# Forms of x at even multiples of 64 bytes with rows 34 to 54 units apart, weights at odd ones; a product of the linear branch's second half moved forward

## The chip, the cores and the metric

The kernel runs on one core of one Trainium2 chip. The metric is the device time of one execution in microseconds (us); runs of one kernel are summarised by their median. TensorE (PE, with its weight loads shown as PEld), VectorE (DVE), ScalarE (ACT) and GpSimd (POOL) work side by side. SyncE (SP) and POOL issue the transfers (DMA) from memory (HBM) into the on-chip buffer. A matmul has two operands there: the stationary one, which is loaded ahead of it, and the moving one, which streams past; its result goes to accumulators that ACT and DVE evacuate.

## The reference

One layer of a decoder: 512 rows of 1,024 numbers with 16 meta rows ahead of them, a retention branch of 4 heads and a gated linear branch (GLA) of 4 heads, merged by sigmoid gates and projected back.

```python
u = rms_norm(h, norm_gain)
proj = u @ w_in
(rq, rk, rv, rg, gq, gk, gv, gg, glr, m_ret, m_gla) = jnp.split(proj, points, axis=-1)
rq = rope(rq, pos); rk = rope(rk, pos) * RET_QK_DIM ** -0.5
o_ret = head_group_norm(retention_chunked(rq, rk, rv), ret_norm_gain) * jax.nn.silu(rg)
log_a = jax.nn.log_sigmoid(glr @ w_gate_up + b_gate) / GLA_GATE_TAU
o_gla = head_rms_norm(gla_chunked(gq * GLA_K_DIM ** -0.5, gk, gv, log_a), gla_norm_gain) * jax.nn.silu(gg)
merged = jax.nn.sigmoid(m_ret) * (o_ret @ w_branch_ret) + jax.nn.sigmoid(m_gla) * (o_gla @ w_branch_gla)
out = rms_norm(h + merged @ w_out, final_norm_gain)[:, N_META:]
```

## The kernel before

**Products in two parts.** Every number of an operand is held as a high part (fp32r) and a low part, the rest. ACT makes the high part by a cast and DVE the low part by a subtraction (`split`, L154), and each product is three matmuls: high by high, high by low, low by high. A matmul multiplies 128 by 128 by 256 (or 264 with 8 meta rows); a few are 512 wide.

**Quads.** `quad` (L257 and following) multiplies x, cut into four blocks of 264 or 256 rows by 512 columns (A11, A12, A21, A22), by a block of weights of 1,024 rows by 512 columns, with 7 products instead of 8 (Strassen's scheme in Winograd's form). Its operands on x's side are seven *forms*: A11, A12, A22 and the sums S1, S2, S3, S4. A product has 24 matmuls (two column tiles by four slices of 128 by three), all of L318, so a quad has 168. Its weights arrive in pieces named w11, w21, x3, x1, w22; some are added up by DVE (L359, L369, L372, L379) or by a transfer that accumulates, issued on POOL (L282). Products are taken in the order A11, A12, S2, S3, S1, A22, S4, and, where `early` is set (the linear branch's projection bg only), A11, S3, S2, A12, S1, A22, S4. Results stand in three accumulators a, b, c: ACT copies one (`copy`, L334), and the caller's `evac` adds.

Two kinds of quad matter. In quads *with rows* (gg0, gg1, gv1; rg0 to rg3 and rv0 to rv3 of the four retention heads; wo1 of the last projection) the form is the stationary operand and the weights move. In the others (gqk1, mr0, mr1, mg0, mg1, rqk0 to rqk3, bg0, bg1) the form moves and the weights are stationary. gq0, gk0, gv0 (L643) at the start and wo0 and wo2 at the end multiply without the scheme; gv0 and wo0 and wo2 have the form stationary too. In the profile xh, xl are the tiles with A11, A12, A22 (and A21) of x, high and low; fh, fl those with the sums; `NAME_h`, `NAME_l` the two parts of a piece of weights; `NAME_a`, `_b`, `_c` the accumulators.

**Where the forms lie.** The pool `cp` gives its tiles out in the order of the code, so that sizes fix addresses. Counted in units of 64 bytes from the start of a partition's row, as worked out from these sizes, before:

| Operand | Start (high part) | From one slice of 128 to the next |
|---|---|---|
| A11, A21, A12, A22 of x | 75, 92, 211, 228 | 34 |
| S1, S2, S3, S4 of x | 619, 687, 755, 823 | 17 |
| the three weight slots, high; low | 1607, 1671, 1735; 1799, 1863, 1927 | 16 |
| forms of bg: A11; A12, S1, S2, S4 | 2081; 2338, 2598, 2730, 2858 | 16 |
| forms of bg in two pieces: S3, A22 | even | 16 |
| forms of wo1 (high parts): A11, A12, A22; S1, S2, S3, S4 | 211, 2293, 2309; 619, 687, 755, 823 | 32; 16 |

The low parts of x's forms lie 272 units further for A and S alike. So A11 and A12 are odd in all slices, A22 and A21 even in all, and the four sums alternate; weights are odd, and so are the high parts of wo1's forms.

**The linear branch's second half.** `gla_branch` runs bg0 and then bg1 over the output of the linear attention. That output arrives in pieces: `gla_sums` forms bg's seven operands (names ga11, ga12, ga22h/l, gs1, gs2, gs3h/l, gs4) step by step while the quads run, with S4's last, after an accumulating transfer into og (L1118, POOL), by a scaled copy on ACT (L1128) and a subtraction on DVE (L1129). `after` fixes the order of two instructions on an engine without a wait. Each engine runs its own list in order; `weave` and the generators' `yield` set how two strands are mixed.

Of the kernel before, what the change touches and what calls it, by code (L numbers as in the profile page):

```python
# [21 lines left out]
F32 = mybir.dt.float32  # L22
# [6 lines left out]
P = 128  # L29
# [18 lines left out]
E_U, E_D, E_A, E_B, E_END, E_ND = range(6)  # L48
A11, A12, A22, S1, S2, S3, S4 = range(7)


# [57 lines left out]
def hybrid_kernel(ctx: ExitStack, tc: tile.TileContext, I, out: bass.AP):  # L109
# [18 lines left out]

    xh = [cp.tile([P, 4, 2, HW], F32R, tag=f"xh{i}", name=f"xh{i}") for i in range(2)]
    xl = [cp.tile([P, 4, 2, HW], F32R, tag=f"xl{i}", name=f"xl{i}") for i in range(2)]  # L130
    ah = {(th, kh): xh[kh][:, :, th] for th in range(2) for kh in range(2)}
    al = {(th, kh): xl[kh][:, :, th] for th in range(2) for kh in range(2)}
    fh = [ah[0, 0], ah[0, 1], ah[1, 1]]
    fl = [al[0, 0], al[0, 1], al[1, 1]]
    fh += [cp.tile([P, 4, HW], F32R, tag=f"fh{i}", name=f"fh{i}") for i in range(3, 7)]
    fl += [cp.tile([P, 4, HW], F32R, tag=f"fl{i}", name=f"fl{i}") for i in range(3, 7)]

# [30 lines left out]
    def vec(ins):  # L168
        return queue("vec", ins)
# [87 lines left out]
    def quad(cols, rows, name, evac, meta=None, adds=True, ahead=False, behind=None, src=None,  # L257
             forms=None, wide=False, sooner=False, early=False):

# [65 lines left out]
        def copy(x, n):  # L325

            y = xc.tile([P, 2, HT], F32, tag="xc", name=f"{name}_x{n}")
            if wide:
                w = HT if n < 3 else 256
                for t in range(2):  # L330
                    nc.scalar.copy(y[:, t, :w], x[t][:, :w])
                return y
            y = y.rearrange("p t c -> p (t c)")[:, :512].rearrange("p (t c) -> p t c", t=2)
            nc.scalar.copy(y, x[2])  # L334
            return y
# [327 lines left out]
    for n in range(NTB):  # L663
        act(nc.scalar.activation(xr[n], xr[n], AF.Square, accum_out=ss[:, n:n + 1]))
        if n == 2:
            for s in range(2):
# [14 lines left out]
                             rt.unsqueeze(2).to_broadcast([P, NTB + 1, P])))  # L681
    vec(nc.vector.scalar_tensor_tensor(u01, u00, -1.0, u01, op0=ALU.mult, op1=ALU.subtract))

    def form(i, x):
        act(nc.scalar.copy(fh[i][:, :, :HT], x))

        def rest():
            vec(nc.vector.tensor_sub(fl[i][:, :, :HT], x, fh[i][:, :, :HT].bitcast(F32)))

        return rest  # L690
# [40 lines left out]
    def forget_gates():  # L731
# [114 lines left out]
    def gla_g(p):  # L846
        sg = g1.tile([P, NTB, 512], F32, tag="gsg", name=f"gsg{p}")
        G["sg", p] = sg

        def evac(n, th, x, y):  # L850
            total(sg[:, 2 * th:2 * th + 2, n * 256:(n + 1) * 256], x, y)

        yield from quad((C_GG + p * 512, C_GG + p * 512 + 256), True, f"gg{p}", evac,
                        sooner=p == 0)

# [244 lines left out]
    def gla_sums():  # L1100
# [24 lines left out]
        gform(A22, a11, list(low))  # L1125
        yield
        hi, lo = gforms[S4]
        after(nc.scalar.mul(hi, a00, -1.0), low[0])  # L1128
# [25 lines left out]
    def gla_branch():  # L1154

        cnt = [0]

        def evac(n, th, p, q):
            pool, tag = ((g1, "gvm"), (g1, "gsum"), (gp, "gk"))[cnt[0] % 3]
            t = pool.tile([P, 2, 256], F32, tag=tag, name=f"gb{cnt[0]}")  # L1160
# [9 lines left out]

        for j in range(2):
            yield from quad((j * 512, j * 512 + 256), False, f"bg{j}", evac, src=I["w_branch_gla"],
                            forms=[[gforms[i][x] for i in range(7)] for x in range(2)], early=True)

# [89 lines left out]
    def ret_g(h):  # L1264
        sg = rp.tile([P, NTB, 512], F32, tag="sg", name=f"sg{h}")
        R["sg", h] = sg
# [3 lines left out]
    def ret_v(h):  # L1270
        vh = rp.tile([P, NTB, 512], F32R, tag="vh", name=f"vh{h}")
        vl = rp.tile([P, NTB, 512], F32R, tag="vl", name=f"vl{h}")
        R["v", h] = vh, vl
# [23 lines left out]
    def ret_scores(h):  # L1297
        qh, ql, kh, kl = R["qk", h]
        dec = rp.tile([P, 2, T], F32, tag="dec", name=f"dec{h}")
        nc.sync.dma_start(dec, I["decay"][h])  # L1300
        sh = rp.tile([P, 1280], F32R, tag="sh", name=f"sh{h}")
        sl = rp.tile([P, 1280], F32R, tag="sl", name=f"sl{h}")
# [26 lines left out]
    def ret_attention(h):  # L1329
# [4 lines left out]
        if h == 0:  # L1334
            nc.gpsimd.memset(rp.tile([P, 16], F32, name="gap"), 0.0)
        oh, ol = [(rp if h < 3 else cp).tile([P, 4, T], F32R, tag=f"o{n}" if h < 3 else f"x{n}0", name=f"o{n}{h}")
                  for n in "hl"]
        R["o", h] = oh, ol
# [109 lines left out]
    for h in range(4):  # L1448
# [14 lines left out]
    mh, ml = [[cp.tile([P, 4, T], F32R, tag=f"x{n}1", name=f"m{n}0"),  # L1463
               rp.tile([P, 4, T], F32R, tag=("sg", "vl")[n == "l"], name=f"m{n}1")] for n in "hl"]
    sums = [[cp.tile([P, 4, 256], F32R, tag=f"f{n}{i}", name=f"ms{n}{i}") for i in range(3, 7)] for n in "hl"]
    mforms = [[m[0][:, :, :256], m[1][:, :, :256], m[1][:, :, 256:], *x] for m, x in zip((mh, ml), sums)]

# [37 lines left out]

    weave(ret_branches(), residual(), skip=14)


# [105 lines left out]
```

## Time and profile before

| | |
|---|---|
| Median of 3 runs | 757.08 us (756.8 to 758.7) |
| The profiled execution's own time | 759.11 us |
| Its span, from the first to the last instruction | 757.3 us |
| TensorE's granted clock, mean | 0.998 |
| HBM over the span | 153 GB/s |

The page gives for each engine its busy time, its share of the span and its count of instructions, and the chain of work that ended last. A row of the timeline is a start, a duration, the engine, the line, the operation and its operands, with the idle time before it and what ended that in brackets. Durations of PE's matmuls overlap, since one is still draining while the next streams; how fast they follow one another is read from their starts. A row of the groups gives a count, the busy time and the mean of one. A row of the windows gives for a stretch each engine's busy time and count.

### The profile page before, as it was taken

The page shows a single profiled execution, that of the slowest core. Times are in us where ns is not written, and L with a number is a line of the kernel's source. Part 1 is how long each engine was busy: PE and PEld are TensorE (multiplying, and loading weights), DVE is VectorE, ACT ScalarE, POOL GpSimd, SP SyncE. Part 2 cuts the span into 40 slices and gives each one's busy share as a digit, 9 for nine tenths or more (in the row PEclk, how much of TensorE's full clock was granted, in tenths as well). Part 3 has the DMA queues.
Part 4 walks back from the last instruction along what each step waited for, and adds up shares of the span by engine and source line. Part 5 has one row for each costly group of instructions (what it writes and reads, how often), then busy time and mean ns, then how long its engine had stood idle before and what let it go on. Part 6 is the DMA issues. An engine that isn't in the chain of part 4 may idle for free.

```text
span 757.3 us, 14065 instructions
## 1 busy us (share of the span) xinstructions
PE 748.2 (99%) x5595; PEld 701.3 (93%) x5595; DVE 609.2 (80%) x873; ACT 450.4 (59%) x764; POOL 138.8 (18%) x173
## 2 busy tenths in 40 slices
PE   9999999999999999999999999999999999999996
PEld 6799899999999999999989999989999999988996
DVE  6699877679897789789957688966787989775994
ACT  7897584666974466556546555646464756532562
POOL 2211110101221122110530100440011210111142
PEclk9999999999999999999999999999999999999999
DMA  9863421821589972733783562795476356687503
GB/s 301 286 141 78 118 63 50 195 85 57 130 182 272 305 165 88 168 112 133 199 249 117 120 159 86 204 223 136 130 166 145 107 144 189 227 194 210 128 29 112
DMA packets 100138, 117.42 MB, mean 155 GB/s; under 512 B 5732, under 2 KB 90852, under 8 KB 99816
## 3 DMA queue, kind: packets, MB, share of 16 engines
q1 hardware_dynamic: 79896, 88.19, 36.7%
q0 software_dynamic: 19888, 27.79, 20.3%
q8 instruction: 44, 0.72, 0.4%
q10 hardware_dynamic: 288, 0.53, 0.2%
q14 instruction: 22, 0.18, 0.1%
HBM read 104.44 MB, written 11.53 MB: 153 GB/s over the span
## 4 chain that ended last, share of the span: by engine, by line
PE 86%; DVE 6%; ACT 2%; DMA 2%; issue 2%; POOL 1%; POOLq 0%; DVEq 0%; ACTq 0%
PE rqk_b L318 6%; PE rv_b L318 6%; PE rg_b L318 6%; PE rqk_c L318 5%; PE br_p L193 3%; PE br_p L189 3%; PE br_p L192 3%; PE gg_b L318 3%; PE gv_p L643 3%; PE mg_b L318 3%; PE rv_c L318 3%; PE rg_c L318 3%; PE mr_b L318 2%; PE bg_b L318 2%; PE gg_c L318 2%
## 5 line engine op out<-in xcount | busy, mean ns | idle before, releaser
L189 PE MATMUL br_p<-oh,br_h 128*128 128x512 f32 x128 | 50.0, 390 | 0.0
L193 PE MATMUL br_p<-oh,br_l 128*128 128x512 f32 x128 | 50.0, 390 | 0.0
L192 PE MATMUL br_p<-ol,br_h 128*128 128x512 f32 x128 | 49.8, 389 | 0.0
L154 ACT CAST rv_h<-rv_w 128x1024 fp32r<-128x1024 f32 x24 | 25.3, 1052 | 27.2 <-DVE rv_w L372 9.6
L154 DVE TENSOR_TENSOR rv_l<-rv_w,rv_h 128x1024 fp32r<-128x1024 f32 x24 | 29.3, 1221 | 9.2 <-ACT rv_h L154 9.2
L154 DVE TENSOR_TENSOR rg_l<-rg_w,rg_h 128x1024 fp32r<-128x1024 f32 x20 | 24.4, 1220 | 8.3 <-ACT rg_h L154 8.3
L154 ACT CAST rg_h<-rg_w 128x1024 fp32r<-128x1024 f32 x20 | 21.0, 1052 | 15.6 <-PE br_p L192 6.0
L282 POOL DMA_DIRECT2D rqk_x<-in_w_in_dram x8 | 10.4, 1302 | 105.4 <-DVE rv_l L154 80.6
L193 PEld LDWEIGHTS br_p<-oh,br_l 128*128 128x128 f32 x128 | 24.0, 188 | 5.2
L192 PEld LDWEIGHTS br_p<-ol,br_h 128*128 128x128 f32 x128 | 24.0, 188 | 4.7
L189 PEld LDWEIGHTS br_p<-oh,br_h 128*128 128x128 f32 x128 | 24.1, 188 | 4.5
L154 ACT CAST rqk_h<-rqk_w 128x1024 fp32r<-128x1024 f32 x20 | 21.1, 1053 | 11.5 <-PE rqk_c L318 2.9
L154 ACT CAST br_h<-br_w 128x1024 fp32r<-128x1024 f32 x16 | 16.8, 1050 | 18.7 <-PE br_p L192 9.5
L154 DVE TENSOR_TENSOR rqk_l<-rqk_w,rqk_h 128x1024 fp32r<-128x1024 f32 x20 | 24.4, 1221 | 3.9 <-ACT rqk_h L154 3.8
L1354 ACT ACTIVATE on<-av,nm,g_r 128x512 f32<-128x512 f32 x16 | 12.5, 779 | 25.3 <-DVE nm L1352 25.3
L318 PE MATMUL rv_b<-rv_l,fh 128*128 128x256 f32 x96 | 27.1, 282 | 0.2 <-DVE rv_l L154 0.2
L318 PE MATMUL rqk_b<-fh,rqk_h 128*128 128x256 f32 (+1 forms) x96 | 27.2, 283 | 0.0
L318 PE MATMUL rqk_b<-fh,rqk_l 128*128 128x256 f32 (+1 forms) x96 | 27.1, 282 | 0.0
L318 PE MATMUL rqk_b<-fl,rqk_h 128*128 128x256 f32 (+1 forms) x96 | 27.1, 282 | 0.0
L318 PE MATMUL rg_b<-rg_h,fl 128*128 128x256 f32 x96 | 27.0, 281 | 0.0
L318 PE MATMUL rv_b<-rv_h,fl 128*128 128x256 f32 x96 | 27.0, 281 | 0.0
L318 PE MATMUL rg_b<-rg_l,fh 128*128 128x256 f32 x96 | 26.9, 280 | 0.0
(721 smaller groups left out, 3260.8 us busy)
## 6 DMA issues: line engine op xcount, KB each, us to landing
rv_w<-in_w_in_dram SPq DMA_DIRECT2D x16, 512.0 KB, 4.2
br_w<-in_w_branch_ret_dram SPq DMA_DIRECT2D x16, 512.0 KB, 3.4
rqk_w<-in_w_in_dram SPq DMA_DIRECT2D x12, 512.0 KB, 4.8
rg_w<-in_w_in_dram SPq DMA_DIRECT2D x12, 512.0 KB, 4.5
rqk_x<-in_w_in_dram SPq DMA_DIRECT2D x8, 512.0 KB, 4.0
rqk_x<-in_w_in_dram POOLq DMA_DIRECT2D x8, 512.0 KB, 8.0
rg_x<-in_w_in_dram SPq DMA_DIRECT2D x8, 512.0 KB, 3.7
rg_x<-in_w_in_dram POOLq DMA_DIRECT2D x8, 512.0 KB, 7.8
```

The source lines that it names most:

```text
L154: return nc.scalar.copy(hi, src), nc.vector.tensor_sub(lo, src, hi.bitcast(F32))
L189: m = nc.tensor.matmul(o, lh, rh, start=first, stop=False)
L192: nc.tensor.matmul(o, lh, rl, start=False, stop=False)
L193: m = nc.tensor.matmul(o, ll, rh, start=False, stop=last)
L282: x = nc.gpsimd.dma_start(t, block(0, 1), accum_op=ALU.add)
L318: m = nc.tensor.matmul(ps[t][:, :n] if wide else ps[t], l, r, start=first and j == 0, stop=kk == 3 and j == 2, skip_group_check=not fresh ...
L643: m = nc.tensor.matmul(pss[t], (al if j == 1 else ah)[t // 2, kh][:, k, c], (lo if j == 2 else hi)[:, kk, :], start=q == kk == j == 0, sto ...
L1354: nc.scalar.activation(on, ps, AF.Identity, scale=r, bias=nm)
```

## The change

Two things change.

First, places. The tiles of x are laid out anew as x0, x1, x2 (high and low of each): x0 holds A11 and A21 (S4 later lies in A21's place), x1 A12, A22 and S1, x2 S2 and S3. Two unused gaps (16 and 112 numbers) shift what follows. Every form starts at an even multiple of 64 bytes, and its slices lie 34 units apart in x0 (A11 at 76, S4 at 94), 54 in x1 (348, 366, 384) and 38 in x2 (780, 798). The weight slots move to 1535, 1599, 1663 and 1727, 1791, 1855, 16 apart, odd as before. bg's forms move by 72 units, so A11's is odd and the others even as before. The merged rows and their sums before the last projection (`mforms`) lie at 348, 2222, 2238, 76, 140, 484 and 780, even too. S1 and S4 of x now hold 256 rows, without the meta rows that they never needed. Since S4 lies in A21's place, it can be made only when gk0 no longer needs A21: its sum (L682 before) goes to another place, and its two parts are made after gg0's fifth product.

Second, the order in bg. bg1's first product (A11) comes ahead of bg0's S2. Its accumulator's copy goes to a tile of its own (`home`), and the evacuated results alternate between two tiles. `gla_sums` yields once more before S4.

The core of the diff:

```diff
+    gap(cp, 16, "gap0")
+    x0, x1, x2 = [[cp.tile([P, 4, w], F32R, tag=f"x{n}{i}", name=f"x{n}{i}") for n in "hl"]
+                  for i, w in enumerate((544, 864, 608))]
+    gap(cp, 112, "gap1")
...
+    fh, fl = [[a[0, 0], a[0, 1], a[1, 1], b[:, :, 576:832], c[:, :, :288], c[:, :, 288:576], z[:, :, 288:]]
+              for a, z, b, c in zip((ah, al), x0, x1, x2)]
...
+            if home and n == 1:
+                y = home()
+                nc.scalar.copy(y, x[2])
+                return y
...
             product(7, S3, x3, c, True)
-            nc.vector.tensor_add(w11, w11, x3)
+            w = nc.vector.tensor_add(w11, w11, x3)
+            if home:
+                after(w, low[1])
...
-    vec(nc.vector.scalar_tensor_tensor(u01, u00, -1.0, u01, op0=ALU.mult, op1=ALU.subtract))
-
-    def form(i, x):
-        act(nc.scalar.copy(fh[i][:, :, :HT], x))
+
+    def form(i, x, prev=None):
+        w = 256 if i in (S1, S4) else HT
+        h, l, x = fh[i][:, :, :w], fl[i][:, :, :w], x[:, :, :w]
+        y = nc.scalar.copy(h, x)
+        if prev:
+            after(y, prev[0])
+        else:
+            act(y)
...
-        forms.append(form(S4, u01))
-        for i in (2, 0, 1, 3):
+        for i in (2, 0, 1):
             forms[i]()
+        vec(nc.vector.scalar_tensor_tensor(u10, u00, -1.0, u01, op0=ALU.mult, op1=ALU.subtract))
...
+        if p == 0:
+            yield from islice(products, 4)
+            next(products)
+            form(S4, u10, low)()
+            yield
...
-            pool, tag = ((g1, "gvm"), (g1, "gsum"), (gp, "gk"))[cnt[0] % 3]
+            pool, tag = (g1, "gvm") if cnt[0] == 5 else ((g1, "gsum"), (gp, "gk"))[cnt[0] % 2]
...
+        def home():
+            return g1.tile([P, 2, 256], F32, tag="gvm", name="bg1_x1")
+
+        def half(j):
+            return quad((j * 512, j * 512 + 256), False, f"bg{j}", partial(evac, j), src=I["w_branch_gla"],
+                        forms=[[gforms[i][x] for i in range(7)] for x in range(2)], early=True,
+                        home=home if j else None)
+
+        a, b = half(0), half(1)
+        yield from run(islice(a, 2), islice(b, 1), a, b)
...
+    def rows4(t, o, w, c):
+        return t[:, o:o + 4 * w].rearrange("p (k c) -> p k c", k=4)[:, :, :c]
+
+    m0 = [cp.tile([P, 3456], F32R, tag=f"x{n}1", name=f"m{n}0") for n in "hl"]
+    mh, ml = [[rows4(t, 0, 544, T), rows4(rp.tile([P, w], F32R, tag=g, name=f"m{n}1"), o, 544, T)]
+              for n, t, g, w, o in zip("hl", m0, ("sg", "vl"), (2304, 2176), (16, 0))]
...
+    for n, m, t in zip("hl", (mh, ml), m0):
+        s23 = cp.tile([P, 2176], F32R, tag=f"x{n}0", name=f"ms{n}0")
+        s4 = cp.tile([P, 2432], F32R, tag=f"x{n}2", name=f"ms{n}2")
+        mforms.append([m[0][:, :, :256], m[1][:, :, :256], m[1][:, :, 256:], rows4(t, 2176, 288, 256),
+                       rows4(s23, 0, 256, 256), rows4(s23, 1024, 256, 256), rows4(s4, 0, 288, 256)])
```

On PE the change of order is one product that moves. Before, where S3 of bg0 ends (gs3h1, gs3l1 by the weights' piece 7), S2 of bg0 follows (gs2 by piece 6):

```order
L318 MATMUL bg0_c_2667<-gs3h1_2507,bg0_7_h_2701 128x256
L318 MATMUL bg0_c_2667<-gs3l1_2509,bg0_7_h_2701 128x256
L318 MATMUL bg0_c_2667<-gs3h1_2507,bg0_7_l_2702 128x256
L318 MATMUL bg0_b_2665<-gs2_2505,bg0_6_h_2730 128x256 x2
L318 MATMUL bg0_b_2665<-gs2_2505,bg0_6_l_2731 128x256
```

After the change, at the same place:

```order
L328 MATMUL bg0_c_2663<-gs3h1_2503,bg0_7_h_2697 128x256
L328 MATMUL bg0_c_2663<-gs3l1_2505,bg0_7_h_2697 128x256
L328 MATMUL bg0_c_2663<-gs3h1_2503,bg0_7_l_2698 128x256
L328 MATMUL bg1_b_2738<-ga11_2497,bg1_1_h_2741 128x256 x2
L328 MATMUL bg1_b_2738<-ga11_2497,bg1_1_l_2742 128x256
```

bg1's A11 (ga11 by bg1's piece 1) stands there now, 24 matmuls of it, and bg0's S2 follows it.

On DVE, in the middle of bg0, before. L369 adds up weights, L154 makes low parts (of ga22, of the weights' pieces 4, 3 and 1), L1167 and L1165 are evacuations, L1129 is S4's form:

```order
L369 TENSOR_TENSOR bg0_w21_2654<-bg0_w21_2654,bg0_w11_2653 128x1024
L154 TENSOR_TENSOR ga22l0_2512<-og1gk_2521,ga22h0_2510 128x512
L154 TENSOR_TENSOR ga22l1_2513<-og1gk_2521,ga22h1_2511 128x512
L1167 TENSOR_TENSOR gb0_2792<-bg0_a_2666,bg0_x1_2696 128x512
L154 TENSOR_TENSOR bg0_4_l_2832<-bg0_w21_2654,bg0_4_h_2831 128x1024
L154 TENSOR_TENSOR bg0_3_l_2860<-bg0_w22_2657,bg0_3_h_2859 128x1024
L1165 SCALAR_TENSOR_TENSOR gb1_2824<-bg0_b_2665,bg0_x3_2795 128x512
L1129 SCALAR_TENSOR_TENSOR gs4_2503<-og0_1331,gs4_2503 128x1024
L154 TENSOR_TENSOR bg1_1_l_2911<-bg1_w11_2895,bg1_1_h_2910 128x1024
```

After the change:

```order
L385 TENSOR_TENSOR bg0_w21_2650<-bg0_w21_2650,bg0_w11_2649 128x1024
L164 TENSOR_TENSOR bg0_5_l_2832<-bg0_x1_2652,bg0_5_h_2831 128x1024
L164 TENSOR_TENSOR ga22l0_2508<-og1gk_2517,ga22h0_2506 128x512
L164 TENSOR_TENSOR bg0_4_l_2873<-bg0_w21_2650,bg0_4_h_2872 128x1024
L164 TENSOR_TENSOR ga22l1_2509<-og1gk_2517,ga22h1_2507 128x512
L1198 TENSOR_TENSOR gb0_2835<-bg0_a_2662,bg0_x1_2692 128x512
L164 TENSOR_TENSOR bg0_3_l_2901<-bg0_w22_2653,bg0_3_h_2900 128x1024
L1160 SCALAR_TENSOR_TENSOR gs4_2499<-og0_1327,gs4_2499 128x1024
L1196 SCALAR_TENSOR_TENSOR gb1_2869<-bg0_b_2661,bg0_x3_2838 128x512
L164 TENSOR_TENSOR bg1_7_l_2937<-bg1_x3_2728,bg1_7_h_2936 128x1024
```

bg1's first split (bg1_1_l), which stood behind S4's form, is gone from here, since it now precedes gs2; bg0's fifth split has come down to this place; and S4's form stands ahead of the evacuation gb1.

On DVE at the start of the kernel, the low parts of the four sums of x, made between gk0's first split and its second, before (fl4, fl3, fl5, fl6 are S2, S1, S3, S4):

```order
L154 TENSOR_TENSOR gk0_0_l_475<-gk0_w0_468,gk0_0_h_474 128x1024
L688 TENSOR_TENSOR fl4_89<-u0_130,fh4_85 128x4x264
L688 TENSOR_TENSOR fl3_88<-u1_131,fh3_84 128x4x264
L688 TENSOR_TENSOR fl5_90<-u0_130,fh5_86 128x4x264
L688 TENSOR_TENSOR fl6_91<-u1_131,fh6_87 128x4x264
```

After the change three of them stand there, and S4's (xl0, in A21's place) stands behind gg0's fifth split:

```order
L164 TENSOR_TENSOR gg0_5_l_940<-gg0_x1_729,gg0_5_h_939 128x1024
L709 TENSOR_TENSOR xl0_82<-u0_126,xh0_81 128x4x256
L164 TENSOR_TENSOR lal01_971<-la_102,lah01_970 128x256
L164 TENSOR_TENSOR gg0_4_l_1015<-gg0_w21_727,gg0_4_h_1014 128x1024
L164 TENSOR_TENSOR gg0_3_l_1084<-gg0_w22_730,gg0_3_h_1083 128x1024
```

It moved past the whole of gk0 and five of gg0's products.

More of the change, by code (lines that the diff above doesn't have):

```diff
@@ L11 @@
 from contextlib import ExitStack
+from functools import partial
 from itertools import islice
@@ L49 @@
 A11, A12, A22, S1, S2, S3, S4 = range(7)
+OH3 = 112
 def constants():
@@ L257, in quad @@
     def quad(cols, rows, name, evac, meta=None, adds=True, ahead=False, behind=None, src=None,
-             forms=None, wide=False, sooner=False, early=False):
+             forms=None, wide=False, sooner=False, early=False, home=None):
         src, forms = src or w_in, forms or (fh, fl)
@@ L851, in evac @@
             total(sg[:, 2 * th:2 * th + 2, n * 256:(n + 1) * 256], x, y)
-        yield from quad((C_GG + p * 512, C_GG + p * 512 + 256), True, f"gg{p}", evac,
-                        sooner=p == 0)
+        products = quad((C_GG + p * 512, C_GG + p * 512 + 256), True, f"gg{p}", evac, sooner=p == 0)
+        if p == 0:
[3 more added lines that the diff above has]
+            yield
+        yield from products
     def gla_qk(p):
@@ L1334, in ret_attention @@
         if h == 0:
-            nc.gpsimd.memset(rp.tile([P, 16], F32, name="gap"), 0.0)
-        oh, ol = [(rp if h < 3 else cp).tile([P, 4, T], F32R, tag=f"o{n}" if h < 3 else f"x{n}0", name=f"o{n}{h}")
-                  for n in "hl"]
+            gap(rp, 16, "gap7")
+        if h < 3:
+            oh, ol = [rp.tile([P, 4, T], F32R, tag=f"o{n}", name=f"o{n}{h}") for n in "hl"]
+        else:
+            oh, ol = [cp.tile([P, 2432], F32R, tag=f"x{n}2", name=f"o{n}{h}")[:, OH3:OH3 + 4 * T]
+                      .rearrange("p (k c) -> p k c", k=4) for n in "hl"]
         R["o", h] = oh, ol
```

34 lines of the change are left out of this document (16 added, 18 removed).

## The prediction

> **What bounds the kernel now.** I read the page first: busy shares, the clock, the chain that ended last; then the waits of PE.
>
> ```profile
> PE 748.2 (99%) x5595; PEld 701.3 (93%) x5595; DVE 609.2 (80%) x873; ACT 450.4 (59%) x764; POOL 138.8 (18%) x173
> PEclk9999999999999999999999999999999999999999
> PE 86%; DVE 6%; ACT 2%; DMA 2%; issue 2%; POOL 1%; POOLq 0%; DVEq 0%; ACTq 0%
> PE bg_b L318 <- DVE gs L1129: 0.9, 1, 0.9
> PE wo_b L318 <- ACT wo_x L334: 0.2, 1, 0.2
> PE rv_b L318 <- DVE rv_l L154: 0.2, 1, 0.2
> ```
>
> TensorE (PE) is busy 99% of the span at full clock, makes 86% of the chain, and its waits are single and small. So the time is the number of matmuls times the pace at which one starts after another, plus a few stalls. The number does not change. What remains is the pace, and the timeline of PE shows that it is not one number. The rows below are first starts of runs of matmuls of the same size (the first column is the start in us); the first row of each next run closes the one before.
>
> ```profile
> 421.73 0.28 PE L318 MATMUL rv_a<-rv_h,xh 128*128 128x256 f32 x1
> 433.12 0.39 PE L503 MATMUL rvm_s<-rvm_h,sel 128*128 128x512 f32 x1
> 433.58 0.28 PE L318 MATMUL rv_c<-rv_h,xh 128*128 128x256 f32 x1
> 434.96 0.28 PE L318 MATMUL rv_c<-rv_h,xh 128*128 128x256 f32 x1
> 436.32 0.28 PE L318 MATMUL rv_b<-rv_h,fh 128*128 128x256 f32 x1
> 439.17 0.28 PE L318 MATMUL rqk_b<-xh,rqk_h 128*128 128x264 f32 x1
> ...
> 221.20 0.39 PE L318 MATMUL bg_a<-ga,bg_h 128*128 128x256 f32 x2
> 223.92 0.39 PE L318 MATMUL bg_b<-gs,bg_h 128*128 128x256 f32 x2
> ...
> 234.07 0.41 PE L318 MATMUL bg_b<-ga,bg_h 128*128 128x256 f32 x2
> 236.96 0.28 PE L318 MATMUL bg_c<-gs3h,bg_h 128*128 128x256 f32 x1
> ```
>
> In the quad rv1, A12, S2, S3 and S1 (96 matmuls, 421.73 to 433.12) take 11.39 us, 118.6 ns each; S4 (24, 436.32 to 439.17) 118.8. A22 between them takes 1.38 us for its first twelve, 115 ns each, and 1.36 for the next twelve, **113.3**. Same line, same types, same size, no idle time. What sets A22 apart is its place: it is the only form of x whose every row starts at an even multiple of 64 bytes. In the linear branch it recurs with the operands' roles exchanged: A12 of bg0, an even form, runs at 2.72/24 = 113.3, and A11 of bg1, an odd form, at (236.96 − 234.07)/24 = 120.4. Weights are odd throughout. The groups by form say it over the four retention heads (second number: mean ns of one):
>
> ```profile
> L318 PE MATMUL rv_c<-rv_h,xh 128*128 128x256 f32 x32 | 8.8, 277 | 0.0
> L318 PE MATMUL rv_c<-rv_l,xh 128*128 128x256 f32 x32 | 8.8, 276 | 0.0
> L318 PE MATMUL rv_b<-rv_h,fl 128*128 128x256 f32 x96 | 27.0, 281 | 0.0
> L318 PE MATMUL rv_b<-rv_l,fh 128*128 128x256 f32 x96 | 27.1, 282 | 0.2 <-DVE rv_l L154 0.2
> L189 PE MATMUL wo_p<-wo_h,mh 128*128 128x256 f32 x64 | 18.0, 281 | 0.0
> ```
>
> rv_c with xh is A22, 276 to 277; the rest stand at 281 to 282. I read this as one form even and one operand odd: fast.
>
> **The change, part by part.** After it all seven forms of x, and those of the merged rows before the last projection, start even with even row pitches; weights stay odd.
>
> *(A) Quads with rows.* In gg0, gg1, gv1, rg0 to rg3 and rv0 to rv3 the form is the stationary operand, as in the rows of rv1. They hold 11 × 168 = 1,848 matmuls. By rv1 a quad's mean is (144 × 118.6 + 12 × 115 + 12 × 113.3)/168 = 118.0, so all at 113.3 would take off 1,848 × 4.7 = 8.7 us. Entering the fast pattern costs 1.38 − 1.36 = 0.02 us in the rows; in gate quads other matmuls come between the products, so I charge one entry to each of 77 products, 1.6 us: **−7.0**. Bounds: 0 and −8.7.
>
> One rule speaks against any of this. The Trainium skill ("TensorE: Matmul & The Clock Gate", "Step-by-step: what each phase is for") gives PE two independent read ports for its two operands, so that a weight load takes nothing from the matmul that runs; by that, where an operand lies would not matter, (A) to (D) would be zero, and the sum −1.6 instead of −10.4. The rows above, 113.3 against 118.6 with no wait between, disagree, and the sum goes by them.
>
> A faster PE asks earlier for its weights' low parts, which DVE makes (L154), and DVE is full in two stages (PE, PEld, DVE, ACT, POOL busy us):
>
> ```profile
> 273.00:295.00 22.00, 22.00 (x203) 21.35 (x205) 22.00 (x29) 16.02 (x24) 8.21 (x4) 1.00 0.37 106
> 586.00:609.00 23.00, 23.00 (x211) 22.26 (x213) 23.00 (x32) 15.95 (x27) 4.93 (x5) 1.00 0.37 115
> ```
>
> The second runs into the rv_b wait of 0.2 us shown above: there DVE is already late, and what rg3 would gain (7.0/11 = 0.64) goes into that wait, plus some of rv3's: **+0.9**. If the first stage and one quad more are lost too, it is 0.64 × 3 = 1.9.
>
> *(B) Last projection.* wo0 and wo2 have 192 matmuls at 281 (the wo_p row) against 276 to 277: 192 × 4.5 = −0.9. wo1 has 168 more at the pace of odd forms, but behind DVE and ACT work of its own (one of PE's waits is there); I count 96 of them, −0.5. Together **−1.4**, bounds 0 and 360 × 4.7 = −1.7.
>
> *(C) Quads where the form moves.* In gq, gk, gqk1, mr, mg and rqk (some 1,700 matmuls) the placing does little:
>
> ```profile
> 353.26 0.28 PE L318 MATMUL mg_a<-xh,mg_h 128*128 128x256 f32 x1
> 356.12 0.39 PE L189 MATMUL br_p<-oh,br_h 128*128 128x512 f32 x1
> ...
> 375.66 0.28 PE L318 MATMUL mg_c<-xh,mg_h 128*128 128x256 f32 x1
> 378.49 0.39 PE L189 MATMUL br_p<-oh,br_h 128*128 128x512 f32 x1
> ```
>
> mg's A12 (odd) takes 2.86 us for 24, 119.2; its A22 (even) 2.83, 117.9. The four sums, whose rows alternate, lie between; so I take half the step, 0.6 ns: **−1.0**, bounds 0 and 1,700 × 1.3 = −2.2. That bg0's moving form falls to 113.3 and mg's does not is what I understand least here; were mg's to follow, some −8 more would be there, yet mg's own even product does not show it.
>
> *(D) gv0*, 96 matmuls 512 wide, half of their forms odd: their row stands at 393 against 390 for the branch, whose operands lie otherwise:
>
> ```profile
> L643 PE MATMUL gv_p<-gv_h,xl 128*128 128x512 f32 x32 | 10.6, 393 | 0.0
> L189 PE MATMUL br_p<-oh,br_h 128*128 128x512 f32 x128 | 50.0, 390 | 0.0
> ```
>
> 96 × 3 ns = **−0.3**, bounds 0 and −1.0.
>
> *(E) The product moved forward.* Before, from 223.92 to 234.07 PE runs S1, A22 and S4 of bg0, 72 matmuls. At 113.3 for S1 and the 117.9 of mg's even product for the others they need 2.72 + 2 × 2.83 = 8.38; they took 10.15, so 1.8 us are stalls. Where they come from:
>
> ```profile
> 227.02 0.39 PE L318 MATMUL bg_c<-ga22h,bg_h 128*128 128x256 f32 x1 [0.21 <-ACT bg_x L334]
> 231.26 0.38 PE L318 MATMUL bg_b<-gs,bg_h 128*128 128x256 f32 x1 [0.88 <-DVE gs L1129]
> 229.98 1.22 DVE L1129 SCALAR_TENSOR_TENSOR gs<-og,gs 128x1024 fp32r<-128x1024 f32 x1 [0.91 <-ACT gs L1128]
> 228.89 1.06 ACT L1128 ACTIVATE gs<-og 128x1024 fp32r<-128x1024 f32 x1 [1.92 <-DMA og<-og1gq]
> 219.78 1.44 POOL L1118 DMA_DIRECT2D og<-og1gq  x1
> ...
> 218.19 0.28 PE L318 MATMUL bg_b<-gs,bg_h 128*128 128x256 f32 x1
> 218.63 1.23 DVE L154 TENSOR_TENSOR ga<-og1gq,ga 128x1024 fp32r<-128x1024 f32 x1 [0.21 <-ACT ga L154]
> 241.54 1.22 DVE L154 TENSOR_TENSOR bg_l<-bg_x,bg_h 128x1024 fp32r<-128x1024 f32 x1 [0.90 <-ACT bg_h L154]
> 245.24 0.39 PE L318 MATMUL bg_b<-gs,bg_h 128*128 128x256 f32 x2
> ```
>
> S4's form hangs on an accumulating transfer that POOL issues at 219.78 and that ends shortly before 228.89 (ACT's wait for it ends there); ACT and DVE need 1.06 and 1.22 more, so it is ready at 231.2. The change puts bg1's A11, 24 × 120.4 = 2.89 us of PE, ahead of bg0's S2; its form has long been there. S4 would stand at 223.92 + 2.72 + 2.83 = 229.47 without stalls, and stands at 232.4 with the product ahead of it: a cover of 1.1 us. A22 moves by as much and loses its 0.21.
>
> What is late next? First bg0's S2, which began at 218.19 and now begins at 221.08. The low part of its weights, third on DVE before, now comes behind bg1's first split, gs2 and ga12, in the place after ga12's row: 218.63 + 1.23 + 1.14 or so, 221.0 (estimated from that row and the spacing of splits). That is as good as no cover. Then bg1's S1, whose split ran from 241.54 to 242.76 while PE came at 245.24: with 1.8 us less ahead of it PE comes at 243.4, a cover of 0.7. I take **−1.6** of the 1.8. Bounds: −1.8; and +0.5, if S2's split comes one operation (1.22) later and bg1's S1 falls behind by its cover once more.
>
> *(F) S4's form of x* is made after gg0's fifth product instead of before gq, since it lies in A21's place. The rows of the fifth product's own split and of S4's first matmul:
>
> ```profile
> 71.93 1.22 DVE L154 TENSOR_TENSOR gg_l<-gg_x,gg_h 128x1024 fp32r<-128x1024 f32 x1
> ...
> 82.77 0.28 PE L318 MATMUL gg_b<-gg_h,fh 128*128 128x256 f32 x1
> ```
>
> Cast and split, 1.06 and 1.22 by the rows of this size above, have 82.77 − 73.15 = 9.6 us. DVE's sum for it is one operation as before, only later. 0, bounds −0.3 and +0.6. POOL's memset is beside everything: 0.
>
> Sum: −7.0 + 0.9 − 1.4 − 1.0 − 0.3 − 1.6 = −10.4. The profiled execution took 759.11 (its span 757.3 and 1.8 around it) and lies 2.0 above the median of the runs, 757.08; against its own time the sum gives 748.7, against the median **746.7**, which I predict, since the result is a median too.
>
> **Rivals.**
> *R1, the pace is gained in part.* DVE binds in more stages (80% busy on average, full in two), or the pattern is lost again after each interruption in the gate quads. If six of the eleven quads give nothing, −10.4 + (6 − 1) × 0.64 = −7.2, 749.9; if also half of (B), 750.6. For it: the full DVE windows. Against: elsewhere DVE has room.
> *R2, the place does not matter*, and A22 is fast for another cause, say as the sixth of seven products. Only (E) is left: 757.08 − 1.6 = 755.5. Against it stand two different products, in two roles, at the same 113.3. It is what the Trainium skill's two ports, named above, would give.
> *R3, slower.* The forms' new pitches of 54 and 38 units have not run. If with them the pattern settles as in bg1's A11, at 120.4, then 2,208 matmuls of (A) and (B) cost 120.4 − 118.0 = 2.4 each: +5.3, less 1.6, 760.8. It makes the kernel slower as soon as the mean in these quads passes 118.0 + 1,600/2,208 = 118.7. Against: the fast A22 has rows 34 apart, even like 38 and 54.
>
> **How the numbers follow.** Forecast 0.75, R1 0.14, R2 0.06, R3 0.05. The forecast's own bounds: with A at −8.7, C at −2.2 and D at −1.0 it is 743.1; with DVE's 1.9 or (E) at +0.5 instead, 747.7 to 748.8. R1 reaches to 750.6 and, with a quad more, 751.2. The range is **743.0 to 751.5**, which leaves out R2 and R3, 0.11. A measurement of this kernel tells some 0.3% (2.3 us) from no change: forecast and R1 are faster, 0.89; R2 is within it, 0.06; R3 is slower, 0.05.
>
> **What would show it.** In the changed profile rv_a, rv_b and rv_c should all stand near 277, rg a little above, mg and rqk hardly moved; PE's wait for gs should be gone; waits for rv_l or rg_l would show DVE as the next bound. If rv_b stays at 281, the reading of the place is wrong; if mg falls to 276 as well, my understanding of the moving form was, and the time will be under 743.

## The result and the profile after

| | before | after |
|---|---|---|
| Median of 5 runs each, us | 757.9 (756.8 to 759.0) | 751.09 (749.87 to 751.72) |
| Ratio of after to before, 95% interval | | 0.9909 (0.9895 to 0.9923) |
| The profiled execution's own time; its span, us | 759.11; 757.3 | 749.87; 748.1 |

The change makes the kernel 0.9% faster, 6.8 us by the medians. Between the two profiled executions it is 9.2. One lies 1.2 above its kernel's median and the other 1.2 below, so some 2.4 us of that difference belong to these two executions and not to the change.

The page of after, engines and chain:

```profile
PE 737.9 (99%) x5595; PEld 691.4 (92%) x5595; DVE 607.4 (81%) x873; ACT 449.9 (60%) x764; POOL 138.4 (18%) x172
PE 85%; DVE 8%; DMA 3%; issue 2%; ACT 1%; POOL 0%; POOLq 0%; DVEq 0%; ACTq 0%
```

The waits of PE (engine and operands, what released it, total us, times, longest):

```profile
PE rg_c L328 <- DVE rg_l L164: 1.1, 2, 0.6
PE wo_c L328 <- DVE wo_l L164: 0.5, 1, 0.5
PE rv_b L328 <- DVE rv_l L164: 0.5, 1, 0.5
```

As many matmuls as before need 10 us less of PE. Its wait for gs is gone, and in place of it stand waits for low parts made by DVE, whose share of the chain rises from 6% to 8%. The pace, from the timeline of PE in rv1 (start in us, duration, operation):

```profile
415.69 0.28 PE L328 MATMUL rv_a<-rv_h,xh 128*128 128x256 f32 x1
...
418.41 0.28 PE L328 MATMUL rv_b<-rv_h,xh 128*128 128x256 f32 x1
...
421.13 0.28 PE L328 MATMUL rv_c<-rv_h,xh 128*128 128x256 f32 x1
...
426.57 0.39 PE L519 MATMUL rvm_s<-rvm_h,sel 128*128 128x512 f32 x1
...
427.03 0.28 PE L328 MATMUL rv_c<-rv_h,xh 128*128 128x256 f32 x1
...
428.45 0.28 PE L328 MATMUL rv_c<-rv_h,xh 128*128 128x256 f32 x1
...
429.83 0.28 PE L328 MATMUL rv_b<-rv_h,xh 128*128 128x256 f32 x1
...
432.55 0.28 PE L328 MATMUL rqk_b<-xh,rqk_h 128*128 128x264 f32 x1
```

A12, S2, S3 and S1 (96 matmuls, 415.69 to 426.57) take 10.88 us, 113.3 ns each, and S4 2.72 for its 24, again 113.3. A22, the fast one of rv1 before, is now the slowest of these: after the two 512-wide matmuls of rvm its first twelve take 1.42 us (118) and the next 1.38 (115). I read this as a pace that has to be entered again after an interruption; in rg1, where matmuls of other shapes come between the products, the first five stand at 114.2 to 114.6. The groups over all heads agree (count, busy us, mean ns of one):

```profile
L328 PE MATMUL rv_a<-rv_h,xh 128*128 128x256 f32 x32 | 8.8, 276 | 0.0
L328 PE MATMUL rv_c<-rv_h,xh 128*128 128x256 f32 x64 | 17.8, 277 | 0.0
L328 PE MATMUL rg_b<-rg_h,xh 128*128 128x256 f32 x128 | 35.4, 277 | 0.0
L199 PE MATMUL wo_p<-wo_h,mh 128*128 128x256 f32 x64 | 17.7, 276 | 0.0
L328 PE MATMUL mg_a<-xh,mg_h 128*128 128x256 f32 x16 | 4.5, 280 | 0.0
L659 PE MATMUL gv_p<-gv_h,xl 128*128 128x512 f32 x32 | 10.6, 393 | 0.0
```

The quads with rows and the last projection stand at 276 to 277 now, not at 281; mg, whose form moves, stays at 280, and gv0 at 393. DVE in the two stages that were full before (PE, PEld, DVE, ACT, POOL busy us; the last three are clock, DMA share and GB/s):

```profile
269.00:291.00 22.00, 21.56 (x204) 20.31 (x202) 22.00 (x29) 15.80 (x24) 8.28 (x4) 1.00 0.36 104
577.00:601.00 24.00, 23.39 (x221) 22.23 (x219) 24.00 (x34) 16.28 (x29) 4.93 (x5) 1.00 0.36 111
```

PE, full in them before, has gaps now (21.56 of 22, 23.39 of 24), while DVE is full throughout. Cut by the first matmul of each stage, the two traces give the ledger (the sum is that of the unrounded rows):

| Term of the forecast | Measured, trace to trace, us | Forecast |
|---|---|---|
| (A) eleven quads with rows: gv1, rv1, rv2 −0.7 each; rv0, rg1, rg2 −0.5 each; gg0, gg1 −0.4 each; rg0, rv3 0; rg3 +0.1 | −4.2 | −7.0 + 0.9 |
| (B) last projection: wo0 −0.44, wo1 +0.04, wo2 −0.43 | −0.8 | −1.4 |
| (C) quads where the form moves, with what lies between | −1.2 | −1.0 |
| (D) up to gq0's first matmul | −1.1 | −0.3 |
| (E) bg0 and bg1 | −1.8 | −1.6 |
| Sum | −9.2 | −10.4 |

### The profile page after: what moved, and what is told of

Same layout as the page of the kernel before. It is cut to its first block, busy times and chain, and to the rows that moved or that the text cites. A ratio compares the mean times of both kernels' runs of the same rounds, so it can differ in the third digit from the quotient of the medians.

```text
span 748.1 us, 14064 instructions
## 1 busy us (share of the span) xinstructions
PE 737.9 (99%) x5595; PEld 691.4 (92%) x5595; DVE 607.4 (81%) x873; ACT 449.9 (60%) x764; POOL 138.4 (18%) x172
## 4 chain that ended last, share of the span: by engine, by line
PE 85%; DVE 8%; DMA 3%; issue 2%; ACT 1%; POOL 0%; POOLq 0%; DVEq 0%; ACTq 0%
PE rv_b L328 6%; PE rqk_b L328 5%; PE rg_b L328 4%; PE br_p L202 4%; PE br_p L203 4%; PE br_p L199 4%; PE rqk_c L328 3%; PE gg_b L328 3%; PE gv_p L659 3%; PE mg_b L328 3%; PE mr_b L328 3%; PE rv_c L328 3%; PE bg_b L328 2%; PE rg_c L328 2%; DMA rg_x<-in_w_in_dram 2%
## 5 line engine op out<-in xcount | busy, mean ns | idle before, releaser
L164 ACT CAST rv_h<-rv_w 128x1024 fp32r<-128x1024 f32 x24 | 25.3, 1053 | 24.5 <-DVE rv_w L388 10.4
L328 PE MATMUL rqk_b<-xh,rqk_h 128*128 128x264 f32 (+1 forms) x128 | 36.2, 283 | 0.0
L328 PE MATMUL rqk_b<-xh,rqk_l 128*128 128x264 f32 (+1 forms) x128 | 36.1, 282 | 0.0
L328 PE MATMUL rqk_b<-xl,rqk_h 128*128 128x264 f32 (+1 forms) x128 | 36.0, 281 | 0.0
L328 PE MATMUL rv_b<-rv_l,xh 128*128 128x256 f32 x128 | 35.5, 278 | 0.5 <-DVE rv_l L164 0.5
L328 PE MATMUL rv_b<-rv_h,xh 128*128 128x256 f32 x128 | 35.8, 280 | 0.0
L328 PE MATMUL rv_b<-rv_h,xl 128*128 128x256 f32 x128 | 35.4, 277 | 0.0
L328 PE MATMUL rg_b<-rg_h,xh 128*128 128x256 f32 x128 | 35.4, 277 | 0.0
L328 PE MATMUL rg_b<-rg_h,xl 128*128 128x256 f32 x128 | 35.4, 276 | 0.0
L328 PE MATMUL rg_b<-rg_l,xh 128*128 128x256 f32 x128 | 35.4, 276 | 0.0
L292 POOL DMA_DIRECT2D rqk_x<-in_w_in_dram x8 | 10.4, 1302 | 103.9 <-DVE vl L164 47.3
```

Of the source, the lines that this page charges most:

```text
L164: return nc.scalar.copy(hi, src), nc.vector.tensor_sub(lo, src, hi.bitcast(F32))
L292: x = nc.gpsimd.dma_start(t, block(0, 1), accum_op=ALU.add)
L328: m = nc.tensor.matmul(ps[t][:, :n] if wide else ps[t], l, r, start=first and j == 0, stop=kk == 3 and j == 2, skip_group_check=not fresh ...
```

## The experiments

**The two halves apart.** `place_only` has the new places and the old order of bg, `order_only` the old places and the new order. Of each edit the core is shown; "..." stands for lines that are not.

```diff
 place_only, against after
...
-        a, b = half(0), half(1)
-        yield from run(islice(a, 2), islice(b, 1), a, b)
+        yield from run(half(0), half(1))
 order_only, against before
...
-        for j in range(2):
-            yield from quad((j * 512, j * 512 + 256), False, f"bg{j}", evac, src=I["w_branch_gla"],
+        a, b = half(0), half(1)
+        yield from run(islice(a, 2), islice(b, 1), a, b)
```

> The new places of x's forms with the old order in the linear branch (bg0 whole, then bg1). If the gain is places plus order and the two add up: quads with rows at 113.3 to 114.6 ns per matmul as after the change, and the stall of PE at bg0's S4 (about 0.9 us, waiting for gs of VectorE) back, with some 1.7 us in all: 752.3 to 753.2. If the order brought most of the gain and the pace only moved the waits: 755 or more.

> The old places with the new order in the linear branch. If places and order add up: quads with rows at 117 to 118.6 ns, no wait of PE for gs in bg0, 1.6 us below the kernel before (756 to 756.5). If the order only pays when PE is faster: as before, 757 to 758.

`place_only`: 751.78 us, ratio 0.9916 (0.9903 to 0.9929). `order_only`: 757.72, ratio 0.9997 (0.9988 to 1.0005), no difference that can be measured: the two halves don't add up as the first case of each expectation has it. Yet each did in its trace what it should. The waits of `place_only`:

```profile
PE bg_b L328 <- DVE gs L1153: 0.9, 1, 0.9
PE rg_c L328 <- DVE rg_l L164: 0.6, 1, 0.6
PE rv_b L328 <- DVE rv_l L164: 0.5, 1, 0.5
```

The wait for gs is back with the old order. In `order_only` it is gone, and bg0's first matmul and rqk0's first stand at

```profile
211.96 0.40 PE L319 MATMUL bg_b<-ga,bg_h 128*128 128x256 f32 x2
251.05 0.28 PE L319 MATMUL rqk_b<-xh,rqk_h 128*128 128x264 f32 x1
```

39.1 us apart, against 253.5 − 212.5 = 41.0 in before. So the places carry the result, 758.0 − 751.8 = 6.2 us, and what the order is worth in a median (0.3 here, 0.7 between `place_only` and after) is less than what its trace shows. With the new places the traces show where a part of it goes. In `place_only` bg takes 41.2 us, and rg0 behind it, from its first matmul to rv0's, 19.14 (272.02 to 291.16), with no wait of PE. In after bg takes 39.2, PE reaches rg0 sooner, waits for rg_l there, and rg0 takes 19.89 (269.16 to 289.05), as much as before (19.91). So in these two traces rg0 gives back 0.75 of the 2.0 that bg saves. To see whether the one trace of each kernel was unusual, both ran once more, unchanged:

> The kernel before, unchanged, for a second profile of another execution. If the 1.8 us of stalls in bg0 belong to the kernel: PE waits some 0.9 us for gs again, and from bg0's first product to rqk0's first 41.0 us pass, as in the first profile. If they were a late transfer in that one execution (its time, 759.11, lay above the 18 others): 39 to 40 us, and 757 to 758.

> The new order with the old places, unchanged, for a second profile. In the first profile bg0's first product to rqk0's first took 39.0 us, and the execution, 756.65, lay 1.1 below its median. If the order gains 2 us in bg and loses them elsewhere in most executions: again 39 us there, and a stall in a later place that the first profile lacks. If bg itself varies: 40 to 41 us.

The stage took 40.6 us in `before_again` (758.73 us in all) and 39.1 in `order_again` (757.0): the saving is there again, and both profiled executions of before lie above its median, both of `order_only` below its own. The other way to remove the wait is to let S4's form not depend on the late transfer. `no_late` is the kernel before with S4's form taken from a10, another of the pieces, so that S4's values are not those of the reference:

```diff
-        after(nc.scalar.mul(hi, a00, -1.0), low[0])
+        after(nc.scalar.mul(hi, a10, -1.0), low[0])
-        after(nc.vector.scalar_tensor_tensor(lo, a00, -1.0, hi.bitcast(F32), op0=ALU.mult, op1=ALU.subtract), low[1])
+        after(nc.vector.scalar_tensor_tensor(lo, a10, -1.0, hi.bitcast(F32), op0=ALU.mult, op1=ALU.subtract), low[1])
```

> The kernel before, with S4's form in the linear branch taken from the data of S1, which are there early, instead of from og after the accumulating transfer (so S4's form holds other values than it should; the transfer itself still runs). If executions without a profile have the same stall at bg0's S4 as the profiled ones: 0.9 to 1.3 us less than before, 756.5 to 757. If the stall is there only under the profiler, or what is gained is lost to late transfers in rqk0 and rg0: within 0.4 us of the kernel before, though its profile shows no wait for gs.

757.57 us, ratio 0.9994 (0.9986 to 1.0003). Its trace has no wait for gs, and the stage takes 252.00 − 211.98 = 40.0, 0.6 to 1.0 less than in the two traces of before. The interval just reaches that 1.0 (0.9987); the interval of `order_only` (from 0.9988) excludes the 1.5 to 1.9 of its traces. So a stall that two traces of before show does not come off the median in full when the order removes it. Why, no run settles: only one execution of each series has a trace, and single runs of `order_only` reach from 755.9 to 759.3.

**What makes a place fast.** The rival to "one form even and one operand odd" is that even starts or the wider row pitches alone do it. Two kernels move the weights and nothing else (a second edit, of `pad`, keeps what lies behind them in place): by 1 unit of 64 bytes (`weights_even`, both operands even) and by 2 (`weights_1mod4`, odd, but another remainder modulo 4).

```diff
 weights_even, against after
-    pad = sp.tile([P, 8], F32, name="pad", bufs=1)
+    pad = sp.tile([P, 24], F32, name="pad", bufs=1)
...
-    gap(cp, 112, "gap1")
+    gap(cp, 96, "gap1")
 weights_1mod4, against after
-    pad = sp.tile([P, 8], F32, name="pad", bufs=1)
+    pad = sp.tile([P, 40], F32, name="pad", bufs=1)
...
-    gap(cp, 112, "gap1")
+    gap(cp, 80, "gap1")
```

> The changed kernel with the weights moved by one unit of 64 bytes, so that weights and forms are both even; all else stays where it is. If what counts is that form and weights differ in parity: quads with rows fall back to 118 to 120 ns, 1,848 + 360 matmuls by 4 to 6 ns, 759 to 763. If an even form is enough, whatever the weights: 113.3 to 114.6 ns as after, 751. bg's A12, S1, S2 and S4 (even) leave 113.3 in the first case too.

> The changed kernel with the weights moved by two units of 64 bytes: odd as before, but 1 past a multiple of 4 instead of 3. If only the parity counts: quads with rows at 113.3 to 114.6, 751. If the fast pattern needs the moving operand in the upper half of four units (2 or 3 past a multiple of four, as all fast products so far have it): 117 to 118 ns, 1,848 x 3.6 = 6.7 us more, 756 to 758.

`weights_even` takes 760.2 us, ratio 1.0029 (1.0017 to 1.0041): the whole gain is gone and 2 us more. Its timeline, A11 of bg1, the one odd form, and later A12 of rv1:

```profile
217.53 0.39 PE L328 MATMUL bg_b<-ga,bg_h 128*128 128x256 f32 x2
...
220.25 0.39 PE L328 MATMUL bg_b<-gs,bg_h 128*128 128x256 f32 x2
...
420.86 0.28 PE L328 MATMUL rv_a<-rv_h,xh 128*128 128x256 f32 x1
...
423.71 0.28 PE L328 MATMUL rv_b<-rv_h,xh 128*128 128x256 f32 x1
```

rv1's A12 is back at 2.85/24 = 118.8 ns with an even form at the new pitch, and bg1's A11, slow before and in after, is at 2.72/24 = 113.3, since its odd form now meets even weights. So the fast pace asks for opposite parity of the two starts, whichever operand is the even one. That this is not enough by itself the quads where the form moves will show. `weights_1mod4` keeps the quads with rows at 113.3 and takes 752.88, ratio 0.9937 (0.9924 to 0.9949); most of its extra time lies in the 512-wide products of the branch, whose matmuls follow one another at 233 ns instead of 227 (384 of them, 2.3 us).

**Why mg stays slow.** mg's operands are of opposite parity too. What differs from rv is that its form, which alternates by 2 units from slice to slice, moves, and its stationary operand lies at the same remainder modulo 4 throughout. `moving2` takes the alternation away (five of x's seven forms at a remainder of 2 in all slices, the odd weights as in after); `moving2_lo` moves besides the low parts of all weights by 2 units, so that the weights alternate between high and low part instead.

```diff
 moving2, against after
...
-                  for i, w in enumerate((544, 864, 608))]
-    gap(cp, 112, "gap1")
+    gap(cp, 32, "gap2")
+              for i, w in ((1, 896), (2, 640))]
+    gap(cp, 16, "gap1")
...
 moving2_lo, against moving2
...
+        if not spaced:
+            spaced.append(gap(wp, 32, "gap3"))
...
```

> In the changed kernel five of the seven forms of x (A12, A22, S1, S2, S3) start at 2 units past a multiple of 4 in every slice (slices 56 and 40 units apart instead of 54 and 38); A11 and S4 stay as they are. If a moving operand runs at 113.3 only when it starts at 2 past a multiple of four (as bg's A12, S1, S2, S4 do, while its S3 and A22 and all of x's forms do not in every slice): in mr, mg and the 256-wide part of rqk those five products fall from 117.8 to 113.3, the 264-wide ones from 121.2 to about 116.7; 600 x 4.5 + 480 x 4.5 = 4.9 us, less what VectorE holds back: 746 to 748. If bg is fast for another cause: 117.8 and 121.2 as after, 751.

> The run moving2 with the low parts of the weights moved by two units, so that the weights' start alternates between 3 and 1 past a multiple of four from matmul to matmul. If the fast pattern is entered when the stationary operand alternates by two units and the moving one does not (as in the quads with rows after the change): in mg, mr and rqk the products A12, A22, S1, S2, S3 fall to 113.3 (256 wide) and 120.0 (264), some 2.9 us; in the quads with rows the moving weights now alternate and their five products go to 117.8 throughout: some 3 us more than moving2 there, 750 to 753 in all. If the role does not matter and any alternation will do: both at 113.3, 745 to 747. If none: as moving2, 751.

`moving2`: 751.11 us, ratio 0.9913 (0.9901 to 0.9926), no better than after. mg stays at 117.8. Of its quads with rows some are fast and some not; A12 of rg1 and A12 of rv1:

```profile
391.09 0.28 PE L330 MATMUL rg_a<-rg_h,xh 128*128 128x256 f32 x1
...
393.91 0.34 PE L201 MATMUL sc<-qh,kh 128*128 128x384 f32 x1
...
416.21 0.28 PE L330 MATMUL rv_a<-rv_h,xh 128*128 128x256 f32 x1
...
418.93 0.28 PE L330 MATMUL rv_b<-rv_h,xh 128*128 128x256 f32 x1
```

Form, pitch, parities and remainders modulo 4 are the same, and the first takes 2.82/24 = 117.5 ns, the second 113.3. `moving2_lo`: 755.29, ratio 0.9964 (0.9951 to 0.9978), with the two kinds of quad exchanged, A12 of mg and A12 of rv1:

```profile
350.97 0.28 PE L334 MATMUL mg_a<-xh,mg_h 128*128 128x256 f32 x1
...
353.69 0.39 PE L201 MATMUL br_p<-oh,br_h 128*128 128x512 f32 x1
...
419.06 0.28 PE L334 MATMUL rv_a<-rv_h,xh 128*128 128x256 f32 x1
...
421.89 0.28 PE L334 MATMUL rv_b<-rv_h,xh 128*128 128x256 f32 x1
```

A12 of mg is at 113.3, A12 of rv1 at 117.9. In all it is slower than every case expected: in its trace the 512-wide products of the branch follow one another at 231 ns, and rg0 takes 1.3 us more than in after. `low_split` tries to have both: after, with the low parts moved only where the weights are stationary.

```diff
-    def wsplit(shape, name):
+    def wsplit(shape, name, o=0):
+        lo = wp.tile([P, 1088], F32R, tag="wlo", name=f"{name}_l", bufs=3)[:, o:o + (512 if len(shape) == 2 else 1024)]
...
-            hi, lo = wsplit([P, 4, 256], f"{name}_{i}")
+            hi, lo = wsplit([P, 4, 256], f"{name}_{i}", 0 if rows else 32)
```

> The changed kernel, but in the quads where the form moves (gqk1, mr, mg, rqk, bg) the low parts of the weights lie 2 units (128 bytes) further, so that the stationary operand's start alternates by 2 units between the matmuls with the high and with the low part; the quads with rows, the branch products and the last projection keep their places. Earlier runs: with both starts constant modulo 4 units two paces were seen (113.3 and 117.8 ns); with the form's slices constant and the low weights shifted everywhere, the quads whose stationary operand alternates went to 114.5 (mg), 115.0 (mr) and 115.4 ns (the 256-wide part of rqk), and those whose moving operand alternates to 117.5. Theory, what decides is that the stationary start alternates, whatever the moving one does: mg 117.8 to about 114.5, mr 117.6 to 115, rqk's 256-wide part 117.2 to 115.4, its 264-wide part 121.1 to 120.5; rows stay at 113.3; 672 x 3.0 + 192 x 1.8 + 600 x 0.6 ns = 2.7 us, so 748.4 against the changed kernel's 751.1. Rival, an alternating moving start costs the pace by itself (the form still alternates by slices here): mg stays at 117.8, and the time at 751.1.

750.48 us, ratio 0.99 (0.9883 to 0.9916): its interval overlaps that of after. A12 of mg:

```profile
349.14 0.28 PE L329 MATMUL mg_a<-xh,mg_h 128*128 128x256 f32 x1
...
351.91 0.39 PE L199 MATMUL br_p<-oh,br_h 128*128 128x512 f32 x1
```

2.77/24 = 115.4 ns, about halfway, and the next five products of mg 116.3 to 117.1; neither theory. Some of what this saved was lost at once, since rg0 now waits longer for DVE: it takes 22.7 us (269.3 to 292.0) where it took 21.7 in after. Put side by side, all with starts of opposite parity but the last row (where a quad is named, A12 of it stands for it, and in `low_split` all products behind its A11):

| Stationary start, modulo 4 units | Moving start | Where | ns per matmul |
|---|---|---|---|
| alternates | constant | after rv1; `moving2_lo` mg | 113.3 |
| alternates | alternates | `low_split` mg | 115.4 to 117.1 |
| constant | alternates | after mg; `moving2_lo` rv1 | 117.9 |
| constant | constant | `moving2` rg1; rv1 | 117.5; 113.3 |
| constant | constant | after bg1: S1; A22; S4 | 113.3; 117.5; 113.8 |
| alternates | constant | `moving2_lo` bg1: A22 | 119.2 |
| same parity | | `weights_even` rv1 | 118.8 |

For x's forms I read the rows so: an alternating stationary start leads into the fast pace, an alternating moving start into the slow one, with both it lies between, and with both constant either can hold. In `moving2` what ran ahead may decide that: rv1's A12 follows A11 directly, rg1's follows six 512-wide matmuls. This is a reading, not a rule, since bg does not obey it. S1, A22 and S4 of bg1 follow one another without a wait (240.71, 243.43, 246.25 to 248.98 in after), all three with both starts constant modulo 4 and of opposite parity, and A22 alone is slow; in `moving2_lo`, where its stationary start alternates, it is slow too. Worked out from the tile sizes, A22's form starts at a multiple of 4 units and those of S1 and S4 at 2 past one; no run moves A22's alone, so the cause stays open. What the runs show is that the fast pace was seen with opposite parity alone.

**Whether DVE took the rest.** `rope_pool` moves the sums of q's rotation in heads 0 and 3 from DVE to POOL. `rope_less` is after without those sums for q and k in these two heads, so that their rotations lack a term.

```diff
 rope_pool
...
-        nc.vector.tensor_sub(m[0], m[0], m[1])
+        (eng or nc.vector).tensor_sub(m[0], m[0], m[1])
...
 rope_less
...
-        nc.vector.tensor_sub(m[0], m[0], m[1])
+        if not less:
+            nc.vector.tensor_sub(m[0], m[0], m[1])
...
```

> In the changed kernel the two sums of the rotation of q of heads 0 and 3 (2 x 0.68 us of VectorE in rg0 and in rg3) go to GpSimd, which is idle there. If VectorE's work holds back rg0, rg3 and rv3: its waits for rg_l and rv_l (1.1 + 0.5 us) shrink by most of that, 749 to 750. If the late transfers hold back rg0: only rg3's part, some 0.7 us, 750.3. If GpSimd slows VectorE or is late for the scores: 751 to 752.

> The changed kernel without the two sums of each rotation (q and k) in heads 0 and 3, 4 x 0.69 us of VectorE less in each of rg0 and rg3 (so q and k of these heads are not rotated as they should). If VectorE is what holds rg0, rg3 and rv3 back: PE's waits for rg_l and rv_l there (1.1 + 0.5 us, with what lies around them 1.9) go, 749.0 to 749.8. If late transfers hold them back: 750.5 to 751.1, and the waits stay.

`rope_pool` is worse than after and than every case expected, 754.96 us, ratio 0.9957 (0.9944 to 0.997). Its largest waits beside the start's:

```profile
PE rg_c L328 <- ACT rg_x L348: 3.0, 1, 3.0
PE rqk_c L328 <- DVE gb L1198: 0.9, 1, 0.9
PE rg_c L328 <- DVE rg_l L164: 0.6, 1, 0.6
```

What it took from DVE came back as longer waits, 3.0 us of one for an accumulator that ACT had not yet copied. `rope_less` takes 750.41, ratio 0.9903 (0.9886 to 0.9921), with single runs from 748.1 to 752.3; the largest waits left in its trace (beside the start's):

```profile
PE wo_c L328 <- DVE wo_l L164: 0.5, 1, 0.5
PE rg_b L328 <- DVE sg L851: 0.5, 1, 0.5
```

and its second window:

```profile
577.00:601.00 24.00, 24.00 (x227) 22.94 (x226) 23.90 (x32) 16.21 (x29) 7.89 (x5) 1.00 0.38 112
```

PE is full again in the second window, its waits for rg_l and rv_l are gone, and rg3 with rv3 takes 46.6 us instead of 48.3. rg0 still takes 21.8 (21.7 in after), with another DVE result (sg) in the place of rg_l, though DVE has 1.65 us free in the first window now (20.35 of 22). So in head 3 DVE's work is what held PE back; in rg0 PE waits for DVE, but taking this work away does not help. In the median 0.7 us of the 1.7 appear, within the spread.

## Why the prediction was right, and where it was not

*The bound and the cause.* Right. The pace of the matmuls set the time and it was the place that set the pace: `weights_even` takes the gain away with one gap, and speeds up the one odd form. R3's slower pace did not come with the new pitches. R2 fails on the same run: if the place did not matter, `weights_even` would equal after, and it is 760.2 against 751.1. That is also what the prediction took from the two independent read ports that the Trainium skill gives PE ("TensorE: Matmul & The Clock Gate", "Step-by-step: what each phase is for"); the measurement decides against that inference.

*(A) Quads with rows.* Mechanism right, size off: −4.2 for −6.1 (the working's own terms, 8.7 less 1.6, give 7.1 and not 7.0). The term that was mis-sized is the give-back, taken as the gain of rg3 and some of rv3, 0.9. The bound named beside it is what came: rg0, rg3 and rv3 gain nothing, and gg0 and gg1, often interrupted, only 0.4 each. `rope_less` shows the wait for DVE in head 3 by taking it away. In rg0 `place_only` shows what the sum lacked: rg0 has its gain there (19.14 us for 19.91) and loses it when the new order brings PE to it sooner, so that (A) and (E) don't add up. The rest I put down to the entry: 0.02 us a product was charged, but twelve matmuls after rvm alone lose 0.06.

*(B) Last projection.* wo0 and wo2 −0.9, as worked out. The −0.5 of wo1 failed: its matmuls did reach 113.6 on average, and what that saved went into the waits for wo_l and wo_x.

*(C) and (D).* (C) is right, −1.2 for −1.0, and mg hardly moved, as foretold. What was understood least there, fast bg0 beside slow mg, is answered in part: mg's form alternates and its stationary operand is the constant one, the slow row of the table. But with the form constant too (`moving2`) mg stays slow, and that stays open. (D) as such is nothing, as the row of gv_p at 393 says. The 1.1 us in this place of the ledger vary from execution to execution with either set of places, so they are luck: gv0's first four matmuls take 2.02 us in the trace of before and 1.01 in that of after, 1.75 in `place_only`, which has after's places, and 1.47 in `order_only`, which has before's. From there to gq0 the traces agree.

*(E) The product moved forward.* Right in the traces of bg, −1.8 for −1.6, with all three covers holding. As a part of the median it was too large: 0.3 us by `order_only` (its interval reaches to 0.9), 0.7 by the difference of after and `place_only`. The working stopped at the end of bg and did not ask what waits behind it; in after that is rg0's 0.75. *(F)* cost nothing that shows.

*The sum.* −10.4 from trace to trace was −9.2, but (D) and the two executions' luck are in that. The medians went down by 6.8, from 757.9, and after lies 4.4 above the 746.7 foretold: by these rows (A) is 1.9 short, wo1 0.5, (D) 0.3 and (E) about 1, while (C) gave 0.2 more; the other 0.8 is the median of before, 757.08 then and 757.9 now. That accounts for the size only roughly, since the ledger is of two executions and the rest of medians. R1's mechanism, DVE binding in more stages, is what happened in three quads, beside the forecast's pace elsewhere.

## What to carry to other kernels

Read the pace from the starts of matmuls, product by product: where equal shapes follow one another at two paces with no wait between, look at where their operands start. For the quads with rows two starts of opposite parity in units of 64 bytes, with the stationary one alternating by 128 bytes, were worth 4.5% of a matmul's time here (113.3 ns for 118.6); weigh such a gain stage by stage against the next engine, since in stages where that one is full it turned into waits here. Do not add two gains that lie one behind the other without asking whether the first brings PE too early to the second, as in rg0. And a stall seen in one execution's trace is not yet a term of the median: run the edit alone before counting on it.

## What the hardware showed beside that

The paces 113.3 and 117.5 ns both occur with the same shapes and the same starts modulo 4: in `moving2` A12 of rg1 and A12 of rv1 hold one each over 24 matmuls. They differ in the weight slot used and in what ran ahead of them. 512-wide matmuls follow places as well, in the branch products from 227 ns in after to 233 in `weights_1mod4`, although their parities there are the same.
